# Epsilon of all norms on VectorE, a differential head's scaling one step later, and the sink's exponential with the maximum as bias

## The chip, the cores and the metric

One NeuronCore of a Trainium2 chip runs the whole kernel in one launch. The metric is device time in microseconds (us) of that core; lower is better. The engines are TensorE (PE, matmuls; PEld is its weight load), VectorE (DVE), ScalarE (ACT), GpSimd (POOL) and SyncE (SP, which issues most of the DMAs).

## The reference, cut to what matters

The function is a trunk of two layers over 256 context tokens and 256 latent tokens of width 1024. Every token passes, in each layer, through three attention mixers (MLA, differential, windowed with a sink), a gated merge, an output projection, and a SwiGLU feed-forward part (FFN). What the change touches are the norms and one softmax:

```python
def rms_norm(x, w):
    y = xf * lax.rsqrt(jnp.mean(xf * xf, axis=-1, keepdims=True) + EPS)
    return (y * w.astype(jnp.float32)).astype(x.dtype)
...
x = x + mx[2] * rms_norm(y, attn_post_norm[l])        # after the output projection
fx = swiglu(modulate(rms_norm(x, ffn_pre_norm[l]), mx[3], mx[4]), ...)
x = x + mx[5] * rms_norm(fx, ffn_post_norm[l])        # after the FFN
kv = rms_norm(ckv, kv_norm) @ w_ukv                   # MLA, 256 wide, the same for cq
o_b = rms_norm(o, norm_w) * (1.0 - lam_init)          # each differential head, 128 wide
p = jax.nn.softmax(jnp.concatenate([s_loc, s_ctx, sink_col], axis=-1), axis=-1)
```

Without its constant factors, each norm is a sum of squares, an epsilon added to it, a power of -1/2, and a multiplication. The softmax of the windowed mixer has one more column, the head's sink, which enters the sum of exponentials only.

## The kernel before, in words

Tokens are handled in four tiles of 128 (tiles 0 and 1 are context, 2 and 3 latent). Projections are split into a high and a low fp32 part and run as three matmuls (L262, L263, L264) on weights that stream from HBM; ScalarE makes the high part (L131, `hl`), VectorE the low one (L132). The order of the matmuls on TensorE and of the DMAs on SyncE is written out by hand. The order on VectorE, ScalarE and GpSimd is made by the framework's scheduler from the order of emission, priorities and a model of costs, so a small edit can move neighbours; each engine then works its list strictly in order.

A norm's row statistic goes through several engines. ScalarE squares and sums (L293). GpSimd adds the epsilon and takes the power -1/2. VectorE, and in one place ScalarE, multiplies. There are these forms:

- `rsqrt` (L283) serves `norm_T`, the norm of MLA's two 256-wide latents, and the differential heads. GpSimd adds at L286 (`rs`) and takes the power at L288 (`rq`). In `norm_T` VectorE then scales at L868 and copies the extra rope columns at L870, TensorE transposes, and the halves are split (ScalarE L880, VectorE L881). In a differential head ScalarE copies the result (L837), GpSimd squares it (L839), VectorE reduces it (L841), and after `rsqrt` VectorE scales it (L843).
- `normed` (L424) is the norm ahead of the FFN and of layer 1. GpSimd adds at L431 (`smn`) and takes the power at L433 (`rn`); VectorE scales one half of the row (L435), ScalarE the other (L436). TensorE transposes (L442), and `modulate_T` applies shift and scale and splits into `hT` (VectorE L455 and L460, ScalarE L457 and L459).
- `residual` (L469) is the norm of an output, added to the stream `xt`. VectorE multiplies both halves by the gate (L475), GpSimd adds (L477, `smy`) and takes the power (L479, `ry`), VectorE adds to the stream (L482, two halves).
- `first_norm` has its own add at L530 on GpSimd, which the change leaves.

In the attention, `attend` (L646) walks over steps, each with parts S (scores), E (softmax), T (transposes), V (values) and F (a head's end), emitted at growing lags. In `softmax_exp` VectorE takes the negated maximum (L669, `nm` or `nmd`; L671 bounds it by the sink), and ScalarE the exponential with that as bias (L673). With a sink, VectorE adds the sink to the negated maximum (L749), ScalarE takes the exponential of that (L750), and VectorE adds it to the sum (L751) and inverts it (L753). For the transposed probabilities ScalarE or VectorE copies `psT` to `pp` (L689, L691), and TensorE multiplies them with the values (L696, L776). L304 are matmuls that only keep TensorE busy.

Of the kernel before, what the change touches and what calls it, by code (L numbers as in the profile page):

```python
# [13 lines left out]
AF = mybir.ActivationFunctionType  # L14
ALU = mybir.AluOpType
# [72 lines left out]
def trunk(ctx: ExitStack, tc: tile.TileContext, x, cx, b_ada, attn_post,  # L88
# [194 lines left out]
    def rsqrt(ss, n, eps_n):  # L283

        r = small([P, n], f"rs{n}")
        nc.gpsimd.tensor_scalar(r, ss, eps_n, None, ALU.add)  # L286
        o = small([P, n], f"rq{n}")
        nc.gpsimd.tensor_tensor(o, r, mhalf[:, :n], ALU.pow)  # L288
        return o
# [135 lines left out]
    def normed(xt):  # L425

        ss = small([P, 2], "ssn", bufs=4)
        for b in range(2):
            sumsq(xt[:, b * 512:(b + 1) * 512], ss[:, b:b + 1])
        sm = small([P, 1], "smn")  # L430
        nc.gpsimd.tensor_scalar(sm, ss[:, 0:1], ss[:, 1:2], D * EPS, ALU.add, ALU.add)  # L431
        r = small([P, 1], "rn")
        nc.gpsimd.tensor_tensor(r, sm, mhalf[:, :1], ALU.pow)  # L433
        xn = [work(), work()]
        nc.vector.tensor_scalar(xn[0], xt[:, :512], r, None, ALU.mult)  # L435
        nc.scalar.activation(xn[1], xt[:, 512:], AF.Copy, scale=r)  # L436
        return xn
# [31 lines left out]
    def residual(t, early, y1, gw, xt):  # L469

        ss, y0 = early
        sumsq(y1, ss[:, 1:2])
        yg = [work(), work()]
        for h, y in enumerate((y0, y1)):
            nc.vector.tensor_tensor(yg[h], y, gw[:, 1 if t < 2 else 0, h * 512:(h + 1) * 512], ALU.mult)  # L475
        sm = small([P, 1], "smy")
        nc.gpsimd.tensor_scalar(sm, ss[:, 0:1], ss[:, 1:2], D * EPS, ALU.add, ALU.add)  # L477
        r = small([P, 1], "ry")
        nc.gpsimd.tensor_tensor(r, sm, mhalf[:, :1], ALU.pow)  # L479
        for h, g in enumerate(yg):  # L480
            hs = slice(h * 512, (h + 1) * 512)
            nc.vector.scalar_tensor_tensor(xt[:, hs], g, r, xt[:, hs], ALU.mult, ALU.add)  # L482
# [163 lines left out]
    def attend(steps, lead=0.0):  # L646
        n = len(steps)
        d, e = steps[0].get("late", 4), steps[0].get("lag", 2)
        for j in range(n + d + 1):
            if j < n:  # L650
                steps[j]["S"]()
            if 0 <= j - 1 < n:
                with tc.high_priority():
                    steps[j - 1]["E"]()
            yield (steps[j]["cost"][0] if j < n else 0.2) + (lead if j < 2 else 0)
            if 0 <= j - e < n and "T" in steps[j - e]:
                with tc.high_priority():
                    steps[j - e]["T"]()
                yield steps[j - e]["cost"][1]
            if 0 <= j - e - 1 < n and "V" in steps[j - e - 1]:  # L660
                steps[j - e - 1]["V"]()
                yield steps[j - e - 1]["cost"][2]
            if 0 <= j - d < n and "F" in steps[j - d]:
                steps[j - d]["F"]()
                yield 0.43
# [32 lines left out]
    def out_T(o, f, oT, qts, scale=None):  # L698

        pt = bank("T")  # L700
        for i, t in enumerate(qts):
            nc.tensor.transpose(pt[:, i * P:(i + 1) * P], o[:, t], ident)
        n = P * len(qts)
        if f % 2 == 0:
            oT.append(s8([P, 2, 2, 512], F32R, "oT"))
        split_into(*[oT[f // 2][:, f % 2, j, 512 - n:512] for j in range(2)], pt[:, :n], scale)
# [10 lines left out]
    def head64_steps(l, env, bn, passes, qk, v, sinks, mask):  # L717
# [3 lines left out]
        for f in range(4):  # L721
            hs = {}
            for t in qts:
                nk = 256 if t < 2 else 512
                pair = {}
                for m in range(2):
# [12 lines left out]
                    def E(st=st, h=h, nk=nk, m=m, pair=pair):  # L739
                        if m == 0:  # L740
                            pair["sm"], pair["nm"] = small([P, 2], "sm2"), small([P, 2], "nm2")
                        sm, nm = pair["sm"], pair["nm"]
                        sk = sinks and [w[:, l * 8 + h - 1:l * 8 + h + 1] for w in (sink, nsink)]
                        softmax_exp(st, st["ps"], nk, sm[:, m:m + 1], nm[:, m:m + 1], nsink[:, l * 8 + h:l * 8 + h + 1] if sinks else None)
                        if m == 0:
                            return
                        if sinks:
                            es = small([P, 2], "es")
                            nc.vector.tensor_tensor(es, nm, sk[0], ALU.add)  # L749
                            nc.scalar.activation(es, es, AF.Exp)  # L750
                            nc.vector.tensor_tensor(sm, sm, es, ALU.add)  # L751
                        rs = small([P, 2], "rsd")
                        nc.vector.reciprocal(rs, sm)  # L753
                        for j in range(2):
                            p = pair[j]["p"][:, :nk]
                            if j:
                                nc.scalar.activation(p, p, AF.Copy, scale=rs[:, j:j + 1])
                            else:
                                nc.vector.tensor_scalar(p, p, rs[:, j:j + 1], None, ALU.mult)  # L759
# [33 lines left out]
    def diff_steps(l, env):  # L793
        qts, nq = env["qts"], len(env["qts"])
        steps = []
        for h in range(4):
            hs = {}
            for i, t in enumerate(qts):
                nk = 256 if t < 2 else 512
                pair = {}  # L800
                for m in range(2):
# [23 lines left out]
                    if m == 1:  # L825
                        def T(st=st, nk=nk):
                            p_T(st, nk, 1)

                        def V(st=st, h=h, nk=nk, i=i, hs=hs):
                            if i == 0:  # L830
                                hs["av"] = bank("V")
                            weigh(st, nk, hs["av"][:, i * P:(i + 1) * P], lambda k: env["dv"][:, k, h * P:(h + 1) * P])
                            if i < nq - 1:
                                return
                            o = hs["o"] = work().rearrange("p (t e) -> p t e", e=P)
                            ob = o[:, qts[0]:4]
                            nc.scalar.copy(ob, hs["av"][:, :P * nq].rearrange("p (t e) -> p t e", e=P))  # L837
                            sq = work().rearrange("p (t e) -> p t e", e=P)
                            nc.gpsimd.tensor_tensor(sq[:, :nq], ob, ob, ALU.mult)  # L839
                            ssd = small([P, 4], "ssd")  # L840
                            nc.vector.tensor_reduce(ssd[:, :nq], sq[:, :nq], AX.X, ALU.add)  # L841
                            rq = rsqrt(ssd[:, :nq], nq, P * EPS)
                            nc.vector.tensor_tensor(ob, ob, rq.rearrange("p (t o) -> p t o", o=1).to_broadcast([P, nq, P]), ALU.mult)  # L843

                        st.update(T=T, V=V)
                        if i == nq - 1:
                            st["F"] = lambda h=h, hs=hs: out_T(hs["o"], h, env["oT", "b"], qts, env["dnw"])
                    steps.append(st)
        return steps
# [687 lines left out]
```

## Time and profile before

| | |
|---|---|
| Time, median of 3 runs | 1478.86 us (1477.71 to 1479.12) |
| Time of the profiled execution | 1479.64 us |
| Its span | 1477.9 us |
| Mean granted TensorE clock | 0.995 |
| PE busy | 1437.3 us (97%) |
| DVE busy | 969.3 us (66%) |
| ACT busy | 684.3 us (46%) |
| POOL busy | 175.8 us (12%) |

The profiled execution is one of its own, with the hardware profiler on; the span is what the profiler saw of it, from the first instruction to the last. The granted clock is 1.0 at TensorE's upper level (2.4 GHz) and 0.5 at its lower one (1.2 GHz). In a row of the timeline the bracket gives how long the engine stood idle before the instruction, and which instruction on which engine ended that.

### The profile page before, as it was taken

How to read it: one execution, taken by the hardware profiler on the slowest of the kernel's cores; microseconds unless marked ns; L12 is line 12 of the kernel's file. 1: busy time of each engine (PE TensorE's matmuls, PEld its weight loads, DVE VectorE, ACT ScalarE, POOL GpSimd, SP SyncE). 2: the span in 40 equal slices, each digit the busy share in tenths (PEclk: the TensorE clock that was granted, in tenths of full speed). 3: DMA queues.
4: the chain of work that ended last, by engine and by line, in shares of the span. 5: the costliest groups of instructions: out<-in, count | busy, mean ns of one | idle time of the engine just before them, and what ended most of it. 6: DMA issues, size and time to landing. Idle time of an engine off the chain costs nothing. (4 is left out here: it accounts for less than half of the span.)

```text
span 1477.9 us, 21889 instructions
## 1 busy us (share of the span) xinstructions
PE 1437.3 (97%) x8434; PEld 1213.7 (82%) x8434; DVE 969.3 (66%) x1646; ACT 684.3 (46%) x1265; POOL 175.8 (12%) x245
## 2 busy tenths in 40 slices
PE   8989999999999999999999999999999899999998
PEld 7867878777777889887778888878798899899986
DVE  4676777878785655879773224779577776666644
ACT  5576554444552355223222123765455655544443
POOL 1262001220000010000000000364013100100000
PEclk9999999999999999999999999999999999999999
DMA  9321322233223542666572324333242426566664
GB/s 351 123 80 43 115 86 100 103 112 128 86 86 129 185 143 98 215 216 213 198 230 99 100 95 151 126 109 130 100 137 90 161 101 221 170 226 217 215 202 161
DMA packets 62728, 216.16 MB, mean 146 GB/s; under 512 B 7048, under 2 KB 7584, under 8 KB 62624
## 3 DMA queue, kind: packets, MB, share of 16 engines
q1 hardware_dynamic: 61184, 210.05, 42.0%
q10 hardware_dynamic: 1440, 4.72, 0.8%
q8 instruction: 66, 1.08, 0.3%
q14 instruction: 38, 0.31, 0.1%
HBM read 209.48 MB, written 5.27 MB: 145 GB/s over the span
## 5 line engine op out<-in xcount | busy, mean ns | idle before, releaser
L262 PE MATMUL psg<-hT,hl 128*128 128x512 f32 (+1 forms) x1328 | 470.6, 354 | 0.0
L264 PE MATMUL psg<-hT,hl 128*128 128x512 f32 (+1 forms) x1328 | 449.2, 338 | 1.0 <-DVE hl L132 1.0
L263 PE MATMUL psg<-hT,hl 128*128 128x512 f32 (+1 forms) x1328 | 448.8, 338 | 0.3 <-DVE hT L460 0.3
L132 DVE TENSOR_TENSOR hl<-raw,hl 128x1024 fp32r<-128x1024 f32 (+2 forms) x251 | 311.0, 1239 | 209.4 <-ACT hl L131 208.7
L131 ACT CAST hl<-raw 128x1024 fp32r<-128x1024 f32 (+2 forms) x251 | 259.3, 1033 | 328.0 <-PE psg L264 172.5
L262 PEld LDWEIGHTS psg<-hT,hl 128*128 128x128 f32 x1328 | 252.4, 190 | 38.6 <-issue 15.4
L264 PEld LDWEIGHTS psg<-hT,hl 128*128 128x128 f32 x1328 | 252.2, 190 | 29.3 <-DVE hl L132 1.4
L263 PEld LDWEIGHTS psg<-hT,hl 128*128 128x128 f32 x1328 | 252.9, 190 | 25.8 <-issue 3.6
L399 DVE SCALAR_TENSOR_TENSOR acc<-aw,siluc,acc 128x512 f32<-128x512 f32 x224 | 165.0, 762 | 22.4 <-DMA aw<-in_ada_rest 21.1
L477 POOL TENSOR_SCALAR smy<-ssy 128x1 f32<-128x1 f32 x12 | 4.1, 339 | 709.7 <-ACT work L293 709.7
L673 ACT ACTIVATE work<-psS,nm 128x512 f32<-128x512 f32 (+1 forms) x96 | 59.1, 616 | 62.2 <-DVE nm L669 34.7
L669 DVE TENSOR_REDUCE nm<-psS 128x1 f32<-128x512 f32 (+1 forms) x96 | 56.9, 596 | 24.5 <-PE psS L735 18.1
L684 PE MATMUL psT<-ca,work 128*128 128x128 f32 x400 | 63.7, 274 | 6.2 <-DVE work L759 3.8
L262 PE MATMUL psg<-oT,hl 128*128 128x512 f32 (+1 forms) x192 | 68.2, 355 | 0.0
L264 PE MATMUL psg<-oT,hl 128*128 128x512 f32 (+1 forms) x192 | 64.9, 338 | 1.6 <-DVE hl L132 1.6
L263 PE MATMUL psg<-oT,hl 128*128 128x512 f32 (+1 forms) x192 | 64.7, 337 | 0.0
L684 PEld LDWEIGHTS psT<-ca,work 128*128 128x128 f32 x400 | 48.6, 141 | 16.9 <-issue 7.0
L262 PE MATMUL psg<-hl,hT 128*128 128x256 f32 (+1 forms) x168 | 57.1, 340 | 1.4 <-ACT hT L131 1.4
L673 ACT ACTIVATE work<-psS,nmd 128x512 f32<-128x512 f32 (+1 forms) x48 | 29.6, 617 | 44.2 <-DVE nmd L669 23.4
L264 PE MATMUL psg<-hl,hT 128*128 128x256 f32 (+1 forms) x168 | 48.0, 285 | 0.4 <-DVE hT L132 0.4
L263 PE MATMUL psg<-hl,hT 128*128 128x256 f32 (+1 forms) x168 | 47.7, 284 | 0.0
L735 PE MATMUL psS<-kT,qT 96*128 96x512 f32 (+1 forms) x96 | 44.0, 541 | 2.7 <-ACT work L673 2.5
(357 smaller groups left out, 2501.8 us busy)
## 6 DMA issues: line engine op xcount, KB each, us to landing
raw<-in_blocks SPq DMA_DIRECT2D x262, 512.0 KB, 3.5
aw<-in_ada_rest SPq DMA_DIRECT2D x80, 512.0 KB, 4.6
aw<-in_ada_first SPq DMA_DIRECT2D x16, 512.0 KB, 7.2
xd<-xt ACTq DMA_DIRECT2D x6, 512.0 KB, 2.7
xt<-xd SPq DMA_DIRECT2D x6, 512.0 KB, 4.5
raw<-in_blocks SPq DMA_DIRECT2D x8, 272.0 KB, 5.8
xt<-in_ctx SPq DMA_DIRECT2D x4, 512.0 KB, 3.8
gw<-row SPq DMA_DIRECT2D x4, 512.0 KB, 4.4
```

What stands on the lines that cost most here:

```text
L131: nc.scalar.copy(hi, src)
L132: nc.vector.tensor_tensor(lo, src, hi.bitcast(F32), ALU.subtract)
L262: nc.tensor.matmul(ps, lhsT=asl(a[0], k), rhs=bsl(b[0], k), start=st, stop=False)
L263: nc.tensor.matmul(ps, lhsT=asl(a[0], k), rhs=bsl(b[1], k), start=False, stop=False)
L264: nc.tensor.matmul(ps, lhsT=asl(a[1], k), rhs=bsl(b[0], k), start=False, stop=en)
L399: nc.vector.scalar_tensor_tensor(acc[:, s], w[:, k], sc, acc[:, s], ALU.mult, ALU.add)
L477: nc.gpsimd.tensor_scalar(sm, ss[:, 0:1], ss[:, 1:2], D * EPS, ALU.add, ALU.add)
L669: nc.vector.tensor_reduce(nm, ps[:, :nk], AX.X, ALU.max, negate=True)
L673: nc.scalar.activation(st["p"][:, :nk], ps[:, :nk], AF.Exp, bias=nm, accum_out=sm)
L684: nc.tensor.transpose(pt[:, k * P:(k + 1) * P], st["p"][:, k * P:(k + 1) * P], ident)
L735: nc.tensor.matmul(st["ps"][:, :nk], lhsT=q, rhs=k, start=z == 0, stop=z == len(ops) - 1 and mk is None)
```

## The change

Three edits stand in one diff. First, the additions of the epsilon at L286, L431 and L477 go from GpSimd to VectorE (22, 10 and 12 instructions); the powers stay on GpSimd. Second, the scaling of a differential head (L843) is taken out of part V and put into a new part G, which `attend` emits a step after V. Third, the two instructions for the sink's exponential (VectorE L749, ScalarE L750, both 128x2) become two ScalarE instructions of 128x1, which read the sink and take the negated maximum as bias (24 pairs).

```diff
     def rsqrt(ss, n, eps_n):
         r = small([P, n], f"rs{n}")
-        nc.gpsimd.tensor_scalar(r, ss, eps_n, None, ALU.add)
+        nc.vector.tensor_scalar(r, ss, eps_n, None, ALU.add)
...
         sm = small([P, 1], "smn")
-        nc.gpsimd.tensor_scalar(sm, ss[:, 0:1], ss[:, 1:2], D * EPS, ALU.add, ALU.add)
+        nc.vector.tensor_scalar(sm, ss[:, 0:1], ss[:, 1:2], D * EPS, ALU.add, ALU.add)
...
         sm = small([P, 1], "smy")
-        nc.gpsimd.tensor_scalar(sm, ss[:, 0:1], ss[:, 1:2], D * EPS, ALU.add, ALU.add)
+        nc.vector.tensor_scalar(sm, ss[:, 0:1], ss[:, 1:2], D * EPS, ALU.add, ALU.add)
...
+            if 0 <= j - e - 2 < n and "G" in steps[j - e - 2]:
+                steps[j - e - 2]["G"]()
...
                             es = small([P, 2], "es")
-                            nc.vector.tensor_tensor(es, nm, sk[0], ALU.add)
-                            nc.scalar.activation(es, es, AF.Exp)
+                            for j in range(2):
+                                nc.scalar.activation(es[:, j:j + 1], sk[0][:, j:j + 1], AF.Exp, bias=nm[:, j:j + 1])
...
                             rq = rsqrt(ssd[:, :nq], nq, P * EPS)
-                            nc.vector.tensor_tensor(ob, ob, rq.rearrange("p (t o) -> p t o", o=1).to_broadcast([P, nq, P]), ALU.mult)
+                            hs["rq"] = rq.rearrange("p (t o) -> p t o", o=1).to_broadcast([P, nq, P])
+
+                        def G(hs=hs):
+                            ob = hs["o"][:, qts[0]:4]
+                            nc.vector.tensor_tensor(ob, ob, hs["rq"], ALU.mult)
...
                         if i == nq - 1:
+                            st["G"] = G
```

Line numbers of the changed kernel are higher from L663 on, by 2 at first and by 7 behind G (L868 becomes L875, L881 becomes L888, L843 becomes L849; L669 becomes L671).

The lists of VectorE show what moved. The first place is the norm of MLA's latents in layer 0 (`norm_T`). In the kernel before, from the fourth tile's scaling on:

```order
L868 TENSOR_SCALAR work<-psT,rq_732 128x256
L870 COPY work<-psT 128x32
L132 TENSOR_TENSOR hl<-raw,hl 128x1024
L868 TENSOR_SCALAR work<-psT,rq_748 128x256
L868 TENSOR_SCALAR work<-psT,rq_757 128x256
L868 TENSOR_SCALAR work<-psV,rq_772 128x256
L881 SCALAR_TENSOR_TENSOR ckvT<-psS,qnw,ckvT 128x128
L132 TENSOR_TENSOR hl<-raw,hl 128x1024
L868 TENSOR_SCALAR work<-psV,rq_781 128x256
```

In the changed kernel, the same place:

```order
L132 TENSOR_TENSOR hl<-raw,hl 128x1024
L286 TENSOR_SCALAR rs_730<-ssn 128x1
L875 TENSOR_SCALAR work<-psT,rq_732 128x256
L877 COPY work<-psT 128x32
L286 TENSOR_SCALAR rs_746<-ssn 128x1
L875 TENSOR_SCALAR work<-psT,rq_748 128x256
L286 TENSOR_SCALAR rs_755<-ssn 128x1
L875 TENSOR_SCALAR work<-psT,rq_757 128x256
L888 SCALAR_TENSOR_TENSOR ckvT<-psS,qnw,ckvT 128x128
L286 TENSOR_SCALAR rs_770<-ssn 128x1
L875 TENSOR_SCALAR work<-psV,rq_772 128x256
L888 SCALAR_TENSOR_TENSOR ckvT<-psS,qnw,ckvT 128x128
```

Each scaling L875 has now an addition `rs` ahead of it, which stands behind the scaling of the tile before, and the low part `hl` (L132) that followed the fourth tile's scaling now stands ahead of that tile's addition.

The second place is the last `residual` ahead of the FFN in layer 1. In the kernel before:

```order
L475 TENSOR_TENSOR work<-psg,gw 128x512 x2
L482 SCALAR_TENSOR_TENSOR xt<-work,ry,xt 128x512 x2
L132 TENSOR_TENSOR hl<-raw,hl 128x1024
L435 TENSOR_SCALAR work<-xt,rn 128x512
L455 TENSOR_SCALAR work<-psT,mod_6739,mod_6929 128x128 x4
```

In the changed kernel:

```order
L475 TENSOR_TENSOR work<-psg,gw 128x512 x2
L477 TENSOR_SCALAR smy<-ssy 128x1
L132 TENSOR_TENSOR hl<-raw,hl 128x1024
L482 SCALAR_TENSOR_TENSOR xt<-work,ry,xt 128x512 x2
L431 TENSOR_SCALAR smn<-ssn 128x1
L435 TENSOR_SCALAR work<-xt,rn 128x512
L455 TENSOR_SCALAR work<-psT,mod_6739,mod_6929 128x128 x4
```

The addition `smy` (L477) stands behind both gate products L475, and the low part `hl` (L132), which stood behind the two L482, stands ahead of them.

The third place is the end of the third differential head in layer 0. In the kernel before:

```order
L841 TENSOR_REDUCE ssd<-work 128x4
L399 SCALAR_TENSOR_TENSOR acc<-aw,siluc,acc 128x512
L818 RECIPROCAL rsd<-sm_3013 128x2
L843 TENSOR_TENSOR work<-work,rq_3030 128x512
L669 TENSOR_REDUCE nmd<-psS 128x1
L819 TENSOR_TENSOR rsd<-rsd,lam 128x1
L399 SCALAR_TENSOR_TENSOR acc<-aw,siluc,acc 128x512
L821 TENSOR_SCALAR work<-work,rsd 128x256
```

In the changed kernel:

```order
L843 TENSOR_REDUCE ssd<-work 128x4
L399 SCALAR_TENSOR_TENSOR acc<-aw,siluc,acc 128x512
L820 RECIPROCAL rsd<-sm_3013 128x2
L286 TENSOR_SCALAR rs_3028<-ssd 128x4
L399 SCALAR_TENSOR_TENSOR acc<-aw,siluc,acc 128x512
L671 TENSOR_REDUCE nmd<-psS 128x1
L821 TENSOR_TENSOR rsd<-rsd,lam 128x1
L849 TENSOR_TENSOR work<-work,rq_3030 128x512
L823 TENSOR_SCALAR work<-work,rsd 128x256
```

The scaling of the head (L843, now L849) went from ahead of the next maximum `nmd` to behind it, and the addition (L286) takes its place ahead.

## Rows read from the trace of the kernel before

**Rows 1.** Page, part 1: busy time (share of the span) xinstructions of each engine.
```profile
PE 1437.3 (97%) x8434; PEld 1213.7 (82%) x8434; DVE 969.3 (66%) x1646; ACT 684.3 (46%) x1265; POOL 175.8 (12%) x245
```

**Rows 2.** Instruction groups by line and form: busy us, mean ns; idle before them, releasers.
```profile
L671 DVE TENSOR_SCALAR nm<-nm,nsink 128x1 f32<-128x1 f32 x48 | 9.9, 210 | 0.8
...
L749 DVE TENSOR_TENSOR es<-nm,sink 128x2 f32<-128x2 f32 x24 | 3.7, 156 | 0.4
...
L673 ACT ACTIVATE work<-psS,nm 128x512 f32<-128x512 f32 x64 | 44.0, 687 | 43.8 <-DVE nm L669 25.0 <-DVE nm L671 17.5 <-DVE acc L399 1.0
...
L689 ACT COPY pp<-psT 128x512 f32<-128x512 f32 x48 | 27.9, 582 | 16.2 <-PE psT L684 15.8
...
L750 ACT ACTIVATE es<-es 128x2 f32<-128x2 f32 x24 | 4.8, 199 | 3.2 <-DVE es L749 3.2
```

**Rows 3.** Timeline, layer-0 norms, POOL and DVE: start us, us, instruction, [idle <-releaser].
```profile
55.18 0.22 POOL L286 TENSOR_SCALAR rs<-ssn 128x1 f32<-128x1 f32 x1
...
55.49 0.57 POOL L288 TENSOR_TENSOR rq<-rs,mhalf 128x1 f32<-128x1 f32 x1
...
56.09 0.48 DVE L868 TENSOR_SCALAR work<-psg,rq 128x256 f32<-128x256 f32 x1 [0.38 <-POOL rq L288]
...
65.21 0.48 DVE L868 TENSOR_SCALAR work<-psV,rq 128x256 f32<-128x256 f32 x1 [0.77 <-POOL rq L288]
```

**Rows 4.** Timeline of PE, MLA's up-projection behind those norms, and its next longer stall.
```profile
79.15 0.38 PE L262 MATMUL psT<-hl,ckvT 128*128 128x256 f32 x1 [1.61 <-DVE cqT L881]
...
97.19 1.22 PE L735 MATMUL psS<-kT,qT 96*128 96x256 f32 x2 [2.49 <-ACT work L673]
```

**Rows 5.** Timeline, third differential head of layer 0: POOL, DVE and PE.
```profile
287.81 1.04 POOL L288 TENSOR_TENSOR rq<-rs,mhalf 128x4 f32<-128x4 f32 x1
...
288.88 0.69 DVE L843 TENSOR_TENSOR work<-work,rq 128x512 f32<-128x512 f32 x1 [1.17 <-POOL rq L288]
...
289.49 0.68 DVE L669 TENSOR_REDUCE nmd<-psS 128x1 f32<-128x512 f32 x1
...
291.36 0.58 PE L696 MATMUL psV<-dv,pp 128*128 128x128 f32 x1 [3.03 <-ACT pp L689]
```

**Rows 6.** Tile rq: who waited for it (us, times).
```profile
  DVE work L843: 8.0, 8
```

**Rows 7.** Timeline, end of layer 0 (down-projection of the last tokens), DVE and PE.
```profile
933.82 0.68 DVE L460 TENSOR_TENSOR hT<-work,hT 128x512 fp32r<-128x512 f32 x1
...
934.41 1.40 DVE L482 SCALAR_TENSOR_TENSOR xt<-work,ry,xt 128x512 f32<-128x512 f32 x2
...
940.73 0.40 PE L262 MATMUL psg<-kept,hT 128*128 128x288 f32 x1 [0.74 <-ACT hT L459]
```

**Rows 8.** Timeline, layer 1, output projection to the FFN.
```profile
1274.22 1.28 DVE L475 TENSOR_TENSOR work<-psg,gw 128x512 f32<-128x512 f32 x2
...
1274.44 0.30 POOL L477 TENSOR_SCALAR smy<-ssy 128x1 f32<-128x1 f32 x1 [5.77 <-ACT work L293]
...
1275.42 1.41 DVE L482 SCALAR_TENSOR_TENSOR xt<-work,ry,xt 128x512 f32<-128x512 f32 x2
...
1276.75 1.22 DVE L132 TENSOR_TENSOR hl<-raw,hl 128x1024 fp32r<-128x1024 f32 x1
...
1279.35 0.33 PE L442 MATMUL psT<-ca,work 128*128 128x128 f32 x1 [0.93 <-DVE work L435]
```

**Rows 9.** Timeline, end of the kernel.
```profile
1472.42 0.69 DVE L475 TENSOR_TENSOR work<-psS,gw 128x512 f32<-128x512 f32 x1 [2.38 <-ACT work L293]
...
1473.47 1.41 DVE L482 SCALAR_TENSOR_TENSOR xt<-work,ry,xt 128x512 f32<-128x512 f32 x2 [0.35 <-POOL ry L479]
```

**Rows 10.** Windows (us, busy of PE, PEld, DVE, ACT, POOL, then PEclk) and one timeline row.
```profile
291.20:294.20 3.00, 2.84 (x9) 2.45 (x10) 3.00 (x6) 1.83 (x4) 0.00 (x0) 0.50 0.00 0
...
1165.80:1168.80 3.00, 3.00 (x22) 2.82 (x23) 2.23 (x8) 2.02 (x7) 0.00 (x0) 1.00 0.35 139
...
1165.79 0.73 PE L735 MATMUL psS<-sk,sQ 128*128 128x512 f32 x2 [1.96 <-ACT work L673]
```

## The prediction

> **What bounds the kernel now.** I read the page's busy times first. TensorE is busy for 1437.3 us of a span of 1477.9 [rows 1], so everything else together can be worth at most the 40.6 us in which it stands idle; VectorE at 66%, ScalarE at 46% and GpSimd at 12% are no bound by their sums. None of the three edits touches a matmul. What they are worth is therefore read only at TensorE's stalls, and at the tail behind its last matmul: a row statistic that comes later costs nothing as long as the transposes that need it come later still. So I went through TensorE's stalls in the timeline, asked of each which chain of small instructions ends it, and laid the changed list of VectorE over that chain. Five places remain in which an edited instruction stands on such a chain; the reader finds them in rows 3 to 9.
>
> **Price of the instructions.** An addition on GpSimd takes 0.22 [rows 3] to 0.30 us [rows 8]; the nearest row on VectorE is the bound by the sink, 128x1, 0.210 us [rows 2]. As a bare price the move is thus worth 0.01 to 0.09 us each, and a hop of the same size (0.08 us) changes sides: rs to rq was on one engine, 0.09 us from end to start [rows 3], and is now between two. The Trainium skill, GPSIMD Engine Reference, introduction, calls GpSimd the wrong engine for ordinary elementwise arithmetic, with VectorE roughly twice as fast. The trace agrees only in part (0.30 against 0.21). By the rule each addition loses about half of its time wherever it stands; what that would make of the time is told with the rivals. The sum goes by the rows and counts position, not price: VectorE works in order, so an addition waits for what stands ahead of it.
>
> **Part 1, norms of MLA's latents, layer 0.** Before, GpSimd runs rs (0.22) and rq (0.57) back to back, ahead of VectorE, and a tile takes 0.22 + 0.57 and two hops of about 0.09, some 0.96 us [rows 3]. In the new list each rs stands behind the previous scaling, which itself waits for its rq: rs 0.21, rq 0.57, scaling 0.48 and two hops make 1.3 to 1.4 us, 0.4 more per tile, for eight tiles. With the low part of 1.22 us (the same form as in [rows 8]) now ahead of the fourth tile, I walk the list to a last scaling at about 67.9 in place of 65.21 [rows 3]: +2.7. VectorE was idle for 0.77 us ahead of that one [rows 3], and I take that much as given back further along the chain (splits, rope on GpSimd) to the matmul at 79.15, which already waits 1.61 us for it [rows 4]. **+1.9**, between 0 (the chain's own waits swallow it) and +3.4 (below).
>
> **Part 2, differential heads.** In the third head of layer 0 VectorE waits 1.17 us for rq and only then takes the maximum nmd at 289.49, on which the exponential, the copy to pp and TensorE's matmul hang, 3.03 us late [rows 5]. With the scaling behind the maximum the wait goes; the addition and one accumulation that was behind take about 0.1 of it: the maximum comes 1.06 us earlier, and the stall shrinks to about 1.97. The rq (1.04 us on GpSimd [rows 5]) is then done about when the scaling is reached, so no new wait. Behind the stall of 3.03 us the granted clock was 0.50 for at least 3.0 us; behind one of 1.96 us it was 1.00 [rows 10]. At half clock 3.0 us of matmuls cost 1.5 us more. So this place gives -1.06 to -2.6; I take **-2.5**, since 1.97 is next to the row with no drop. All eight waits of this kind sum to 8.0 us [rows 6]; the other seven stand at no long stall of TensorE, and for the small ones in layer 1 I take **-0.4** (0 to -1.2).
>
> **Part 3, sink.** VectorE loses 24 instructions of 0.156 us; ScalarE trades 24 of 0.199 for 48 [rows 2]. A pointer as bias is priced by two 128x512 rows that read PSUM: 0.687 with it, 0.582 without [rows 2], so one of the 48 takes 0.20 to 0.30 us. ScalarE pays +4.8 to +9.6 us in sum, in idle time of an engine at 46%; it no longer waits for L749 (3.2 us in 24 [rows 2]). On the chain to the transposes the gain of 0.156 stands against one more small exponential: **-0.1**, between -0.5 and +1.0.
>
> **Part 4, end of layer 0.** In the list of VectorE the sum smy now follows the two gate products and a low part of hT. At the tile whose matmul waits 0.74 us at 940.73, that low part ends at 934.50, so smy ends near 934.6, ry (0.56, as the other powers) near 935.2, and the addition to the stream starts at 935.26 in place of 934.41 [rows 7]: +0.85, less 0.18 since smn on VectorE is shorter by a hop and 0.1. +0.7 reaches the stalled matmul. The next tile has a low part hl of 1.22 us between smy and its two additions; I take half of it as in hand and add +0.6 (an estimate): **+1.3** (+0.5 to +2.0).
>
> **Part 5, layer 1 ahead of the FFN.** Before, smy ran at 1274.44, beside the second gate product [rows 8]. Now it follows both products (1275.42 to 1275.63), and the low part hl of 1.22 us stands ahead of the additions to the stream, which therefore start at 1276.70 in place of 1275.42: +1.28. smn gives 0.2 back. The transposes at 1279.35, already 0.93 us late [rows 8], come **+1.05** later (+0.4 to +2.6).
>
> **Part 6, tail.** The last gate product ends at 1473.11; smy on VectorE comes behind it instead of beside it, and the last additions start at about 1473.9, not at 1473.47 [rows 9]. Nothing hides this: **+0.45** (+0.3 to +0.7).
>
> **Sum.** 1.9 - 2.5 - 0.4 - 0.1 + 1.3 + 1.05 + 0.45 = +1.7 us on the profiled execution of 1479.64, or 1481.34. That execution lies 0.78 us above the median of 1478.86; against the median the forecast is 1480.6 us, +0.12%. A measurement of this kernel tells about 0.2%, 3 us, from no change; by that the forecast is "no change", on the slow side. Its own range, with some of the bounds above going each way, is 1478 to 1483.5.
>
> **The rivals.**
>
> *Slower, by the clock.* Two stalls grow: the one at 79.15 from 1.61 to 3.5 us, the one at 1279.35 from 0.93 to 2.0; and the head's stall ends at 1.97. Between 1.96 us (no drop) and 3.03 us (drop) [rows 10] the rows leave open where the clock falls; 2.49 us at 97.19 [rows 4] also stands ahead of a slow matmul (1.22 us for two of 128x256). If it falls from about 2 us, part 1 costs 1.9 + 1.5, part 5 1.05 + 1.5, and part 2 gives 1.06 only: 3.4 - 1.06 - 0.4 - 0.1 + 1.3 + 2.55 + 0.45 = +6.1, that is 1485.0. For it: the first of these lies beyond 3.03. Against it: the stall at 97.19 follows within 20 us and is set by other engines, so it can take up what TensorE loses there; and matmuls of L304, which keep TensorE busy, stand ahead of the other.
>
> *Faster, by shorter chains.* VectorE reaches most additions without a queue: part 1 costs 0, because tiles wait for ScalarE's squares anyway, part 4 gives 0.2, part 5 costs 0.4, and the heads give all, 2.5 + 1.2, the sink 0.5. With the tail's +0.45 that is -3.55, or 1475.3. The GPSIMD page of the Trainium skill, in the place named above, would have it this way. For it: the 8.0 us of waits for rq [rows 6]; against: the lists, in which rs stands behind a scaling that waits.
>
> *Nothing arrives.* The later statistics fall into TensorE's slack, and the head's stall is taken over by the next thing (its copy to pp on ScalarE): -1.0 and +0.45, 1478.3.
>
> **How the numbers follow.** Forecast 0.48, of which 0.38 lies within 0.2% and 0.10 above; slower by the clock 0.22; faster 0.18; nothing 0.12, of which 0.10 within and 0.02 above. That makes faster 0.18, same 0.48, slower 0.34. The range reaches from the faster rival to just past the slower one, 1475.0 to 1486.0, and leaves out the ends of both.
>
> **What would show it.** In the changed profile: the last latent scaling near 67.9 and a stall of 3 to 3.5 us in place of 1.61 [rows 4]; the head's stall near 2.0 and no half clock behind it [rows 5]; the stall at the FFN of layer 1 near 2.0 [rows 8]; the last additions 0.45 us further behind the last gate product's start [rows 9]. The forecast is wrong if the latent stall keeps its length (then 1479 or less), or if the head's stall keeps its 3 us (then 1483 or more), or if TensorE shows half-clock stretches behind stalls that were short before.

## The result and the profile after

The changed kernel takes 1486.45 us (median of 6 runs, 1484.74 to 1492.74), the kernel before 1478.8 us in the same comparison: 1.0058 times as long, 95% interval 1.004 to 1.0075. The medians lie 7.7 us apart; the ratio, which is not that of the two medians, makes it 8.6 us. Forecast was 1480.6 us, 1.7 us above the kernel before, with a range up to 1486.0. The change is slower, by four to five times what the forecast gave. The profiled execution after took 1485.24 us (span 1483.4) against 1479.64, so it shows 5.6 us of the loss.

Part 1 of the page after, to be laid beside [rows 1]:

```profile
PE 1436.9 (97%) x8434; PEld 1215.3 (82%) x8434; DVE 971.7 (66%) x1666; ACT 690.7 (47%) x1289; POOL 165.3 (11%) x201
```

No engine does much more work, and TensorE does the same. The loss is waiting, as in the prediction, and it has to be looked for in TensorE's stalls. Since the order of TensorE's matmuls is written by hand and is the same in both kernels, the start of each matmul can be set against the start of the same matmul before. The difference, after minus before, at a few places (half clock is a stretch at a granted clock of 0.50):

| Start in the kernel before (us) | Lag after (us) | What lies between this row and the one above |
|---|---|---|
| 68 | +0.4 | |
| 94 | +3.5 | MLA's latent norms of layer 0, half clock behind them |
| 104 | -0.5 | the stall that was at 97.19 [rows 4] and its half clock |
| 286 | -0.9 | first and second differential head |
| 296 | -3.7 | third head |
| 322 | -2.3 | fourth head |
| 560 | -2.2 | windowed heads with sinks, merge |
| 580 | -1.5 | ahead of the FFN of layer 0 |
| 930 | -1.5 | FFN of layer 0 |
| 965 | +2.6 | end of layer 0, start of layer 1 |
| 1155 | +1.8 | attention of layer 1 |
| 1175 | +3.0 | half clock behind a stall that is as long as before |
| 1275 | +3.3 | |
| 1290 | +5.7 | ahead of the FFN of layer 1 |
| last matmul | +5.1 | |
| end of the span | +5.5 | tail |

The stalls that answer to [rows 4], [rows 5], [rows 7] and [rows 8], in the timeline of TensorE after (start us, us, instruction, idle before it and its releaser):

```profile
81.56 0.39 PE L262 MATMUL psT<-hl,ckvT 128*128 128x256 f32 x1 [2.13 <-DVE cqT L888]
...
289.08 0.71 PE L698 MATMUL psV<-dv,pp 128*128 128x128 f32 x4 [1.78 <-ACT pp L691]
...
316.51 0.63 PE L704 MATMUL psT<-ca,work 128*128 128x128 f32 x4 [0.57 <-DVE work L849]
...
940.74 0.41 PE L262 MATMUL psg<-kept,hT 128*128 128x288 f32 x1 [2.20 <-ACT hT L459]
...
949.70 0.66 PE L442 MATMUL psT<-ca,work 128*128 128x128 f32 x4 [0.92 <-DVE work L435]
...
1284.16 0.88 PE L442 MATMUL psT<-ca,work 128*128 128x128 f32 x4 [2.46 <-DVE work L435]
```

The latent stall went from 1.61 to 2.13 us (with a new one of 1.29 us ahead of it, at 70.97), the third head's from 3.03 to 1.78, the one at the end of layer 0 from 0.74 to 2.20, the one ahead of the FFN of layer 1 from 0.93 to 2.46. Two of these have no counterpart before: the one on the fourth head's scaling (L849), and the one at 949.70.

A part of the largest of these can be seen on GpSimd. The place of [rows 8], after:

```profile
1278.70 0.20 DVE L477 TENSOR_SCALAR smy<-ssy 128x1 f32<-128x1 f32 x1
...
1278.82 1.22 DVE L132 TENSOR_TENSOR hl<-raw,hl 128x1024 fp32r<-128x1024 f32 x1
...
1278.98 1.46 POOL L479 TENSOR_TENSOR ry<-smy,mhalf 128x1 f32<-128x1 f32 x1 [6.51 <-DVE smy L477]
...
1280.48 1.42 DVE L482 SCALAR_TENSOR_TENSOR xt<-work,ry,xt 128x512 f32<-128x512 f32 x2 [0.44 <-POOL ry L479]
```

Here `ry` on GpSimd takes 1.46 us, not 0.56: it starts beside the low part `hl` (L132) and ends 0.40 us behind it. The additions to the stream (L482) stood 1.20 us behind the first gate product before [rows 8]; now they stand 2.98 us behind it (it starts at 1277.50). The last `residual` of layer 0 shows the same:

```profile
944.34 1.22 DVE L132 TENSOR_TENSOR hl<-raw,hl 128x1024 fp32r<-128x1024 f32 x1
...
944.44 1.53 POOL L479 TENSOR_TENSOR ry<-smy,mhalf 128x1 f32<-128x1 f32 x1 [6.76 <-DVE smy L477]
```

The view by tile `ry` gives the whole:

```profile
L479 POOL TENSOR_TENSOR ry<-smy,mhalf x12: 550/552/1535, 529.9 to 1478.5; 128x1 f32<-128x1 f32 x12
...
  DVE xt L482: 7.6, 12
```

Nine of the twelve `ry` take 0.55 us and three take 1.4 to 1.53 us; these are the three with an `hl` behind `smy` in VectorE's list. And VectorE now waits at all twelve for `ry`, 7.6 us together.

### The profile page after: what moved, and what is told of

Its sections match the earlier page's. It is cut to its first block, busy times and chain, and to the rows that moved or that the text cites. A ratio compares the mean times of both kernels' runs of the same rounds, so it can differ in the third digit from the quotient of the medians.

```text
span 1483.4 us, 21867 instructions
## 1 busy us (share of the span) xinstructions
PE 1436.9 (97%) x8434; PEld 1215.3 (82%) x8434; DVE 971.7 (66%) x1666; ACT 690.7 (47%) x1289; POOL 165.3 (11%) x201
## 5 line engine op out<-in xcount | busy, mean ns | idle before, releaser
L132 DVE TENSOR_TENSOR hl<-raw,hl 128x1024 fp32r<-128x1024 f32 (+2 forms) x251 | 310.1, 1236 | 205.9 <-ACT hl L131 205.3
L479 POOL TENSOR_TENSOR ry<-smy,mhalf 128x1 f32<-128x1 f32 x12 | 9.4, 781 | 722.1 <-DVE smy L477 722.1
L671 DVE TENSOR_REDUCE nm<-psS 128x1 f32<-128x512 f32 (+1 forms) x96 | 57.0, 597 | 27.8 <-PE psS L737 17.2
L691 ACT COPY pp<-psT 128x512 f32<-128x512 f32 (+1 forms) x72 | 36.8, 510 | 19.2 <-PE psT L686 18.8
```

The lines of the kernel that those rows point to most:

```text
L132: nc.vector.tensor_tensor(lo, src, hi.bitcast(F32), ALU.subtract)
L671: nc.vector.tensor_reduce(nm, ps[:, :nk], AX.X, ALU.max, negate=True)
L691: nc.scalar.copy(dst, src)
```

## The experiments

The theory tested (A): the loss is `smy`. Moved to VectorE, it lets the scheduler put `hl` between `smy` and the additions that need `ry`, and the power on GpSimd stands still while VectorE runs this instruction with two SBUF operands. Rivals: the latent norms and the clock behind them (B), every moved addition a little (C), VectorE as the place of `smy` as such (D). Times are medians with the kernel before timed on the same chip beside them.

**The additions of `rsqrt` alone.** Edit, on the kernel before:

```diff
         r = small([P, n], f"rs{n}")
-        nc.gpsimd.tensor_scalar(r, ss, eps_n, None, ALU.add)
+        nc.vector.tensor_scalar(r, ss, eps_n, None, ALU.add)
```

> Only the 22 additions of rsqrt (L286) on VectorE, all else as before. Theory A (the loss sits in smy): the first latent norms come about 1.5 us later at TensorE's 69 us and the time is within 2 us of before, since the later stall at 97 us takes that up; the rq waits of the heads shift little. Rival B (the latent norms and a half-clock stretch behind them are the loss): +3 us or more. Rival C (all additions cost alike, half of the 44 moved here): about +3.5 us.

Measured: 1478.68 us against 1478.67, ratio 0.9996 (0.9987 to 1.0006). That is theory A's number and neither rival's; but it is a sum of opposites. Latents cost, as in the change; the third head gains (below).

**`smy` alone.**

```diff
         sm = small([P, 1], "smy")
-        nc.gpsimd.tensor_scalar(sm, ss[:, 0:1], ss[:, 1:2], D * EPS, ALU.add, ALU.add)
+        nc.vector.tensor_scalar(sm, ss[:, 0:1], ss[:, 1:2], D * EPS, ALU.add, ALU.add)
```

> Only the 12 additions smy (L477) on VectorE. Theory A: VectorE's list puts a low part hl (L132, two SBUF operands) between smy and the two additions to the stream at three places, and ry on GpSimd beside it takes 1.4 to 1.5 us instead of 0.56; about +4 us at the end of layer 0, +1.5 ahead of the FFN of layer 1 with half clock behind it, +0.8 ahead of the FFN of layer 0, +0.5 at the tail: +5 to +8 us, nearly the whole loss of the change. Rival B: +2 us. Rival C: 12 of 44, about +2 us.

Measured: 1486.22 us against 1478.67, ratio 1.0045 (1.0033 to 1.0057): 12 of the 44 additions bring most or all of the loss of the change.

**The change without `smy`.** The changed kernel, with the line above put back on GpSimd.

> The changed kernel with smy (L477) back on GpSimd. Theory A: 0 to -3 us against before, since the heads' gain of 2 to 3 us is left and little stands against it. Rival B and rival C: +4 to +5 us against before.

Measured: 1479.86 us against 1478.67, ratio 1.0006 (0.9993 to 1.0019). The loss is gone; a gain over the kernel before, which theory A left room for, is not there.

**`smy` between the gate products.** The changed kernel; the addition stays on VectorE and is emitted ahead of the second product.

```diff
+        sm = small([P, 1], "smy")
+        r = small([P, 1], "ry")
         for h, y in enumerate((y0, y1)):
+            if h:
+                nc.vector.tensor_scalar(sm, ss[:, 0:1], ss[:, 1:2], D * EPS, ALU.add, ALU.add)
+                nc.gpsimd.tensor_tensor(r, sm, mhalf[:, :1], ALU.pow)
             nc.vector.tensor_tensor(yg[h], y, gw[...], ALU.mult)
-        sm = small([P, 1], "smy")
-        nc.vector.tensor_scalar(sm, ss[:, 0:1], ss[:, 1:2], D * EPS, ALU.add, ALU.add)
-        r = small([P, 1], "ry")
-        nc.gpsimd.tensor_tensor(r, sm, mhalf[:, :1], ALU.pow)
```

> The changed kernel with smy emitted between the two gate products; it stays on VectorE, and its list then has the second gate product (one operand in PSUM) behind smy and the low part hl behind the additions to the stream. Theory A (the place of hl beside ry decides, not the engine of smy): ry takes 0.56 us again at all 12 places, time 0 to -3 us against before. Rival D (smy on VectorE costs by itself, through hops and the engine's queue): +4 us or more, ry as before the edit or not.

Measured: 1479.68 us against 1478.67, ratio 1.0001 (0.999 to 1.0011). The tile `ry`, and the place of [rows 8], in this run:

```profile
L479 POOL TENSOR_TENSOR ry<-smy,mhalf x12: 548/550/922, 528.8 to 1471.2; 128x1 f32<-128x1 f32 x12
...
1273.74 0.68 DVE L480 TENSOR_TENSOR work<-psg,gw 128x512 f32<-128x512 f32 x1
...
1273.90 0.55 POOL L479 TENSOR_TENSOR ry<-smy,mhalf 128x1 f32<-128x1 f32 x1 [6.73 <-DVE smy L478]
...
1274.48 1.41 DVE L483 SCALAR_TENSOR_TENSOR xt<-work,ry,xt 128x512 f32<-128x512 f32 x2
```

`ry` runs beside the second gate product, which has one operand in PSUM, in 0.55 us, and the additions start 1.47 us behind the first gate product's start at 1273.01. One of the twelve takes 0.92 us, so the expectation of 0.56 at all twelve was one short; in VectorE's list one `smy` has the low part of hT (L460, two SBUF operands) behind it. With the same engines and the same instructions, only their order differs from the change, so it is not VectorE as the engine of `smy` that costs, and rival D falls as far as that goes. But two things change here at once: `hl` no longer stands behind `smy`, and `ry` runs beside the second gate product again and not behind it. Which of them counts, this run does not tell; the next two bear on it.

**What stretches `ry`.** Two kernels with `smy` alone on VectorE, and one instruction behind it that nobody needs, in the place that `hl` had. In the first it reads one SBUF tile, in the second two:

```diff
         nc.gpsimd.tensor_tensor(r, sm, mhalf[:, :1], ALU.pow)
+        nc.vector.tensor_reduce(small([P, 1], "dum"), yg[0], AX.X, ALU.max)
```

```diff
         nc.gpsimd.tensor_tensor(r, sm, mhalf[:, :1], ALU.pow)
+        nc.vector.tensor_tensor(work(), yg[0], xt[:, :512], ALU.mult)
```

> smy on VectorE as in the run e3_smy, and behind it on VectorE one more instruction that nobody needs: a maximum over 512 columns of one SBUF tile (tensor_reduce, about 0.68 us, one operand). It takes the place in VectorE's list in which hl stood. If the partner's two SBUF operands are what stretches ry, ry takes 0.55 to 0.6 us at all 12 places, though VectorE is busy beside it. If any busy VectorE stretches it, ry takes 0.8 us or more.

> The same, with the instruction that nobody needs a product of two SBUF tiles of 512 columns (tensor_tensor, about 0.69 us, two operands). If two SBUF operands are what stretches ry, ry takes 0.9 to 1.1 us at all 12 places: it ends some 0.4 us behind the product. If not, 0.56 us as in the run with one operand.

Measured, tile `ry` in the run with one operand:

```profile
L479 POOL TENSOR_TENSOR ry<-smy,mhalf x12: 548/550/559, 532.0 to 1478.7; 128x1 f32<-128x1 f32 x12
```

In the run with two:

```profile
L479 POOL TENSOR_TENSOR ry<-smy,mhalf x12: 924/927/937, 535.9 to 1489.3; 128x1 f32<-128x1 f32 x12
...
  DVE xt L483: 5.3, 12
```

Both added instructions last 0.68 us and start 0.12 us behind the start of `smy`. Beside the one with one operand all twelve `ry` take 0.55 us (0.548 to 0.559); beside the one with two all twelve take 0.93 us (0.924 to 0.937). So it is not VectorE being busy. The two instructions differ in more than the operands (a maximum writes one column, a product 512), but the second gate product is a product too and writes 512 columns, with one operand in PSUM, and `ry` beside it took 0.55 us (above): what is left is the second SBUF operand. It counts which of the two starts first: over all profiles but these two, 13 powers of 128x1 began while a VectorE instruction with two SBUF operands ran, and all of them ended 0.40 to 0.45 us behind it; 14 began 0.14 to 0.37 us ahead of one, and they took 0.55 to 0.57 us. The times are 1484.91 us (ratio 1.003, 1.0013 to 1.0047) and 1495.01 us (1.0105, 1.0084 to 1.0127), against 1478.55. The 10 us between them are more than twelve times 0.38 us. The product also takes a `work` buffer from the pool that the norm uses; what that adds was not taken apart.

The run with one operand says something of the cause, too. In it no `ry` is stretched, no `hl` stands behind `smy`, and the additions to the stream follow `ry` at once, 1.47 us behind the second gate product's start, where the kernel before has 0.60 to 1.21: `ry` now begins only behind that product. The run is still 6.4 us slower by the medians, 0.13 to 0.47% by the ratio (from four runs), against 7.6 us and 0.33 to 0.57% for `smy` alone. The added maximum keeps VectorE no longer than `ry` does (0.07 us of idle time are left ahead of the additions); what it moves elsewhere is not known. Two of TensorE's stalls and the additions ahead of the second, with one operand:

```profile
942.53 0.41 PE L262 MATMUL psg<-kept,hT 128*128 128x288 f32 x1 [2.50 <-ACT hT L459]
...
1281.34 1.41 DVE L483 SCALAR_TENSOR_TENSOR xt<-work,ry,xt 128x512 f32<-128x512 f32 x2
...
1285.28 0.66 PE L442 MATMUL psT<-ca,work 128*128 128x128 f32 x4 [1.82 <-DVE work L435]
```

With `smy` alone:

```profile
943.18 0.40 PE L262 MATMUL psg<-kept,hT 128*128 128x288 f32 x1 [2.49 <-ACT hT L459]
...
1285.98 1.00 PE L442 MATMUL psT<-ca,work 128*128 128x128 f32 x4 [2.64 <-DVE work L435]
```

The stall at the end of layer 0, 0.74 us before, is the same with and without `hl` and a stretched `ry`. The one ahead of the FFN of layer 1, 0.93 us before, grows by 0.9 us from the place of `smy` and by another 0.8 from `hl` and the stretch; there the additions stand 2.06 us behind the first gate product's start (1279.28), against 1.20 before and 2.98 in the change. So theory A is right that `smy` is the loss, but `hl` and the stretched power are the smaller part of it. The greater part, as far as these stalls show it, is that `smy` stands behind both gate products, so that `ry`, hidden beside the second one before, is waited for. The two intervals overlap, and the exact shares stay open.

**Part G alone.** All additions stay on GpSimd (the part of the diff on G).

> Only part G (the scaling of a differential head emitted a step later), all additions on GpSimd. The prediction's part 2 gave this edit the gain of 2.5 us at the third head of layer 0; but VectorE's list shows the scaling of that head unmoved ahead of the maximum when the addition stays on GpSimd. Theory A: no gain there, the 3 us stall stays, time within 1 us of before. As the prediction put it: -2.5 to -3 us.

Measured: 1477.83 us against 1478.55, ratio 0.9988 (0.9976 to 1.0). The third head, in its timeline:

```profile
286.22 0.69 DVE L849 TENSOR_TENSOR work<-work,rq 128x512 f32<-128x512 f32 x1 [1.17 <-POOL rq L288]
...
286.83 0.68 DVE L671 TENSOR_REDUCE nmd<-psS 128x1 f32<-128x512 f32 x1
...
288.70 1.14 PE L698 MATMUL psV<-dv,pp 128*128 128x128 f32 x4 [2.54 <-ACT pp L691]
```

The scaling (L849) still stands ahead of the maximum (L671) and still waits 1.17 us for `rq`, as in [rows 5]; the stall is 2.54 us, half a microsecond shorter than before, which the expectation had not. In the run with the additions of `rsqrt` alone, without G, the same place reads:

```profile
286.09 0.68 DVE L669 TENSOR_REDUCE nmd<-psS 128x1 f32<-128x512 f32 x1
...
287.08 0.69 DVE L843 TENSOR_TENSOR work<-work,rq 128x512 f32<-128x512 f32 x1 [0.24 <-POOL rq L288]
...
287.96 0.71 PE L696 MATMUL psV<-dv,pp 128*128 128x128 f32 x4 [1.85 <-ACT pp L689]
```

There the maximum comes first and the scaling waits 0.24 us. The order that helps the third head comes with the addition on VectorE, not with G.

**The sink alone.** The two lines of the sink from the diff, all else as before.

> Only the sink's exponential with the maximum as bias. Theory A: one small exponential takes 0.2 to 0.3 us, TensorE's stalls in the windowed heads of layer 0 move by less than 1 us each way, time within 1.5 us of before. A rival by which the 24 more instructions on ScalarE are paid in full: +5 us or more.

Measured: 1479.75 us against 1478.55, ratio 1.0 (0.999 to 1.0011). One of the small exponentials takes 0.28 us.

**`smn` alone.** The addition L431 on VectorE.

> Only the 10 additions smn (L431) on VectorE; VectorE's list is otherwise that of before. Theory A: each norm ahead of a projection starts some 0.2 us earlier, which TensorE sees at two of its stalls: 0 to -0.6 us, within the noise. Rival C (every moved addition costs): about +2 us.

Measured: 1479.94 us against 1480.08, ratio 0.9999 (0.9986 to 1.0012).

**The parts that help, together.** Part G, `smn`, and this, on the kernel before:

```diff
-    def rsqrt(ss, n, eps_n):
+    def rsqrt(ss, n, eps_n, eng=None):
...
-        nc.gpsimd.tensor_scalar(r, ss, eps_n, None, ALU.add)
+        (eng or nc.gpsimd).tensor_scalar(r, ss, eps_n, None, ALU.add)
...
-                            rq = rsqrt(ssd[:, :nq], nq, P * EPS)
+                            rq = rsqrt(ssd[:, :nq], nq, P * EPS, nc.vector)
```

> Part G, smn on VectorE, and the additions of rsqrt on VectorE in the differential heads alone; smy, the latent norms and the sink as before. Theory A: the third head's stall shrinks from 3.0 to about 1.8 us (-1.3, and -1.5 more where no half clock follows), small stalls in the heads of layer 1 shrink (-0.6), smn gives -0.4; the fourth head's scaling comes +0.7 later as in the change: -1 to -3 us against before, faster than before and than the change. Rival: what the head gives at 288 us is taken back by the fourth head's own chain and by stalls that are set by DMA and GpSimd: 0.

Measured: 1476.22 us against 1480.08, ratio 0.9973 (0.996 to 0.9986). It is 3.9 us faster than the kernel before (2.1 to 5.9 by the interval), more than the 1 to 3 us expected, and the only kernel here that is clearly so; for part G alone the interval touches 1.

**The change once more**, on the chip of the last two.

> The changed kernel once more, on the same chip as the two runs above, for the size of its loss: +5 to +8 us against before.

Measured: 1486.14 us against 1480.08, ratio 1.0049 (1.0032 to 1.0067).

## Why the prediction was wrong, point by point

The direction within its range, that later statistics cost more than the head gives, was right; the size was not. At the end of the span the lag is +5.5 us, where the sum had +1.7; part 4 alone is 2.8 of what was missing, and the other misses go both ways. By the prediction's own parts:

**Part 1, latents: right in size, not in where it shows.** The walk through the list gave a last scaling near 67.9:

```profile
68.16 0.48 DVE L875 TENSOR_SCALAR work<-psV,rq 128x256 f32<-128x256 f32 x1 [0.47 <-POOL rq L288]
```

TensorE came +2.07 us later by the matmul at 79.15 (lag +0.34 at 68, +2.41 there), forecast was +1.9. It does not come as one stall of 3 to 3.5 us in place of 1.61, but as 1.29 at 70.97 and 2.13. That it is swallowed at the stall of 97.19, as the table above suggests, is mostly the clock: the profiled execution before ran the stretch behind that stall at the lower level (1.2 GHz, columns as in [rows 10]),

```profile
96.60:102.60 6.00, 5.41 (x13) 4.15 (x14) 1.85 (x6) 3.84 (x12) 0.03 (x1) 0.50 0.24 87
```

while a run without the latents' edit (the parts that help) had the same stall and no drop:

```profile
96.60:102.60 6.00, 5.99 (x26) 4.60 (x27) 3.54 (x11) 5.60 (x14) 0.36 (x1) 1.00 0.24 87
...
96.61 0.70 PE L737 MATMUL psS<-kT,qT 96*128 96x256 f32 x2 [2.48 <-ACT work L675]
```

Between 30 and 104 us this run gained 2.9 us on the kernel before, and the change in its second profile, with a stall of 2.49 us and no drop either, gained 0.9: the latents cost 2.0 us.

**Part 2, third head: right in mechanism, in size partly by luck.** The lag moves by -2.8 us there (-0.9 to -3.7), forecast was -2.5, with a stall of 1.78 us and no half clock behind it. The prediction put it to the scaling "behind the maximum", and that is the order that helps; it did not say which edit makes the order, and the runs show that G alone leaves the scaling ahead and that the addition on VectorE moves it. The clock's share was luck: in the change without `smy` and in the run with `smy` between the products the same stall, of 1.89 and 1.88 us, was followed by a granted clock of 0.50, and the lag moved by 1.0 to 1.1 us only. The fourth head was missing from the sum. There the rope on GpSimd (L642) now stands ahead of `rq`:

```profile
313.21 0.16 DVE L286 TENSOR_SCALAR rs<-ssd 128x4 f32<-128x4 f32 x1
...
313.40 0.74 POOL L642 TENSOR_TENSOR rsh<-rsh,cb 128x256 f32<-128x256 f32 x1 [1.18 <-DVE rs L286]
...
314.10 1.02 POOL L288 TENSOR_TENSOR rq<-rs,mhalf 128x4 f32<-128x4 f32 x1
...
315.15 1.22 DVE L849 TENSOR_TENSOR work<-work,rq 128x512 f32<-128x512 f32 x1 [1.46 <-POOL rq L288]
```

`rs` ended at 313.37, `rq` started only behind the rope's 0.74 us, and TensorE's transposes waited for L849 (316.51, above). With an earlier stall at the same head that was set by a chain through GpSimd's rope and ScalarE, the third head's gain shrank by 1.4 us.

**Parts 3 and 6: nothing against the sink, tail right.** Between 322 and 560 us, where the heads with sinks lie, the lag moved by +0.1 us, forecast -0.1; both are far within the noise of the run with the sink alone. In the tail,

```profile
1477.51 0.69 DVE L475 TENSOR_TENSOR work<-psS,gw 128x512 f32<-128x512 f32 x1 [1.95 <-ACT work L293]
...
1479.06 1.41 DVE L482 SCALAR_TENSOR_TENSOR xt<-work,ry,xt 128x512 f32<-128x512 f32 x2 [0.73 <-POOL ry L479]
```

the additions stand 1.55 us behind the last gate product's start; before it was 1.05 [rows 9]. That is +0.50, forecast +0.45.

**Part 4, end of layer 0: the step that failed.** Forecast +1.3 (0.7 to the matmul at 940.73, and 0.6 for the tile behind it, half of whose delay was "in hand"). The lag went from -1.45 to +2.60, +4.05: 1.46 at 940.73, 1.09 at 949.70 and 1.5 behind that. Three things were missing.

First, "ry (0.56, as the other powers)" was taken as a fixed price. At the last tile, where "a low part hl of 1.22 us" stands behind `smy`, `ry` took 1.53 us, so the additions started behind `hl` by 0.45 us more, and that tile's stall (949.70, 0.92 us) did not exist before. They stood 3.13 us behind the second gate product's start, against 1.21 before: 1.92 us later, not the 1.22 of `hl`. The trace of the kernel before held a warning that small instructions on GpSimd have no fixed price; there one of the twelve `smy`, beside an `hl`, took 0.75 us and not 0.30:

```profile
1263.28 1.23 DVE L132 TENSOR_TENSOR hl<-raw,hl 128x1024 fp32r<-128x1024 f32 x1 [0.25 <-ACT hl L131]
...
1263.93 0.75 POOL L477 TENSOR_SCALAR smy<-ssy 128x1 f32<-128x1 f32 x1 [50.13 <-ACT work L293]
```

Second, each tile was costed by itself, but the tiles hang together through VectorE's list. Two tiles ahead of the last one, in the kernel before (times of each execution's own clock; TensorE runs 1.5 us earlier in the changed one):

```profile
927.63 1.42 DVE L482 SCALAR_TENSOR_TENSOR xt<-work,ry,xt 128x512 f32<-128x512 f32 x2 [0.35 <-POOL ry L479]
...
930.94 0.49 DVE L435 TENSOR_SCALAR work<-xt,rn 128x512 f32<-128x512 f32 x1 [1.89 <-POOL rn L433]
```

And after:

```profile
926.08 0.20 DVE L477 TENSOR_SCALAR smy<-ssy 128x1 f32<-128x1 f32 x1
...
927.01 1.42 DVE L482 SCALAR_TENSOR_TENSOR xt<-work,ry,xt 128x512 f32<-128x512 f32 x2 [0.73 <-POOL ry L479]
...
930.16 0.49 DVE L435 TENSOR_SCALAR work<-xt,rn 128x512 f32<-128x512 f32 x1 [0.66 <-POOL rn L433]
```

L435 came 0.78 us earlier after, where TensorE was 1.5 us earlier: this tile was already 0.7 us late, and the one behind it added its own 0.8. The stall at 940.73 grew by 1.46 us, forecast was 0.7. No `ry` is stretched at these two tiles (0.55 us); it is the later place of `smy`, paid at each tile.

Third, the norms of the latents in layer 1 also have their addition on VectorE, behind four instructions of the modulation; part 1 looked at layer 0 alone. With the additions of `rsqrt` alone the lag rises by 0.9 us between 930 and 965. The 1.5 us are not theirs alone: with `smy` alone, which leaves these norms as they were, the lag grows by 0.8 us at the same matmuls.

The same `ry` took 1.40 us ahead of the FFN of layer 0 and made a stall of 0.55 us where there was none: +0.7, not in the sum.

**Part 5, ahead of the FFN of layer 1: the same step.** "The additions to the stream, which therefore start at 1276.70" took `ry` as hidden beside `hl`. The rows above show it ending 0.40 us behind. The stall grew by 1.53 us, forecast +1.05. In the profiled execution it was followed by half clock, and the lag grew by 0.9 us more until 1283; in the change's second profile the same stall of 2.46 us was followed by a granted clock of 1.00, and it grew by 0.4.

**The rivals.** The slower rival's time, 1485.0 us, was the nearest, but its mechanism, the clock behind the two grown stalls, is not the cause. Behind the latents and ahead of the FFN of layer 1 the clock did fall in the change's first profile (the second place is shown in the last section), and it fell at neither in its second. The first profile, behind the latents:

```profile
83.40:86.40 3.00, 3.00 (x14) 2.90 (x14) 2.94 (x6) 2.93 (x6) 2.86 (x3) 0.50 0.18 48
```

The second profile, at both places:

```profile
81.20:87.20 6.00, 6.00 (x38) 5.47 (x39) 5.87 (x15) 5.89 (x10) 5.71 (x8) 1.00 0.16 36
...
1286.80:1289.80 3.00, 3.00 (x25) 2.78 (x25) 2.28 (x6) 1.54 (x5) 0.00 (x0) 1.00 0.43 173
```

Yet the span of the second is the longer one, 7.7 us over the kernel before against 5.5. The additions of `rsqrt` alone have the latent stall, too, and cost nothing in sum, and `smy` alone, which leaves the latents as they were, brings 7 us. The rule of the Trainium skill, GPSIMD Engine Reference, introduction, gave a faster kernel through cheaper additions; the additions are cheaper (0.20 us, against 0.30) and the kernel is slower. The rule that bore on the stretched `ry` was another: the Trainium skill, SBUF — State Buffer, section "Who interferes with whom", states that a VectorE instruction with two SBUF inputs contends with a GpSimd instruction that reads SBUF, and that one with a single input (outside its two-port modes) does not. The trace agrees with both halves: 0.93 us beside two operands, 0.55 beside one. The prediction read that `ry` takes 0.56 us in the kernel before, and not beside what: at the place of [rows 8] it ran beside the second gate product, which has one operand in PSUM.

## What to carry to other kernels

The price of an instruction on GpSimd is read together with what VectorE does beside it: beside a VectorE instruction with two SBUF operands a power of 0.55 us lasted until some 0.4 us behind that instruction's end. A small instruction that moves onto the engine that waits for its result stands in that engine's order: here it came behind both gate products, the power behind it was no longer hidden, and what the scheduler put into the gap was paid on top. Emitting it one instruction earlier (between the gate products) took the cost away without changing engines. A list of edits is timed one by one: here one cost 7 us, and a part of another, joined with two that cost nothing, gave 4.

## What the runs showed of the hardware that was not expected

The length of a stall alone does not tell whether the clock falls behind it. Behind 1.96 us it stayed at 1.00 before [rows 10] and fell in the changed kernel, at the same matmul, where the stall is as long (first and last row; the second is the place ahead of the FFN of layer 1):

```profile
1167.80:1170.80 3.00, 3.00 (x14) 2.72 (x15) 1.61 (x6) 2.13 (x8) 0.00 (x0) 0.60 0.27 105
...
1284.20:1287.20 3.00, 3.00 (x16) 3.00 (x17) 2.09 (x6) 1.33 (x4) 0.00 (x0) 0.54 0.47 190
...
1167.63 0.73 PE L737 MATMUL psS<-sk,sQ 128*128 128x512 f32 x2 [1.96 <-ACT work L675]
```

A granted clock of 0.60 and 0.54 over these 3 us says that most of them ran at the lower level. All 13 profiles of this case have that stall of 1.96 us; behind it the clock fell in eight and stayed in five. Behind 2.20 us (940.74) it did not fall, behind 2.46 us (1284.16) it did in one profile of the changed kernel and did not in the other, and behind 2.48 us it did not in the run of the parts that help (above). So the prediction's search for a length between 1.96 and 3.03 us had no answer in single profiles.

The spread of one kernel's runs goes with the clock. Of the change's first six runs the fastest, 1484.74 us, had a mean granted clock of 0.995 and the slowest, 1492.74 us, 0.989; of 29 runs of the kernel before, the fastest, 1475.08 us, had 0.998 and the slowest, 1482.98 us, 0.992. Most of the loss of the change does not come from it: on the chip of the last three experiments, the runs with a mean of 0.995 have a median of 1479.66 us before and 1484.82 us for the change.
